# Three of eight inner pairs of a gate-and-up group by seven block products, with half of the weight sums made by an accumulating DMA

## The chip, the cores and the metric

The kernel runs on one core of one Trainium2 chip. TensorE multiplies, VectorE (DVE) and ScalarE (ACT) work on tiles in SBUF and read the PSUM banks, GpSimd (POOL) here only issues DMAs by software, SyncE (SP) issues DMAs by hardware. The metric is the device time of one execution in microseconds. All data are float32; TensorE works on pairs of rounded parts (below).

## The reference, cut to what matters

One encoder block over 256 tokens of width 2048: four mixers, an attention over a memory of 256 rows, and a gated feed-forward. The change touches only the first half of the last line, the product of the normed tokens with `w_gate_up` (2048 x 11264):

```python
x = x + mix @ w_out[l]
x = x + cross_attention(rms_norm(x, norm_g[l, 1]), mem_n, w_xq[l], w_xkv[l], w_xo[l])
x = x + swiglu(rms_norm(x, norm_g[l, 2]), w_gate_up[l], w_down[l])

def swiglu(h, w_gate_up, w_down):
    gate, up = jnp.split(h @ w_gate_up, 2, axis=-1)
    return (jax.nn.silu(gate) * up) @ w_down
```

## The kernel before, in words

**Weights.** All weight matrices are cut on the host into blocks of 128 x 128, in the order in which they are used, and laid into one array `W` of 252 slabs. A slab is 16 blocks, 128 partitions x 2048 floats, 1 MB. `Stream` brings them in. SP loads a slab into one of three `raw` buffers (line 81). Each half slab (1024 columns) is then split in two: ScalarE copies it rounded to `wh` (line 102), VectorE subtracts to get the rest `wl` (line 103). The pool `wp` holds three such halves. `take` hands out four blocks (512 columns) at a time, and before the first block of each half it has the next two halves made as well; with the pool `extra` open it would be three, with a fourth buffer.

**Products.** The tokens are held transposed, as 16 slots of 128 inner rows, each split the same way: `slot[:, 0:256]` the rounded part of all 256 tokens, `slot[:, 256:512]` the rest. A block product of 128 tokens with 512 columns over 128 inner rows is therefore three matmuls, hi x wh, hi x wl, lo x wh (`part_rows`, lines 349 to 351), all into one PSUM bank.

**Gate and up.** `gate_up` walks over 11 groups of 512 gate columns and the 512 up columns that belong to them. For a group, `gemm_rows` makes the gate columns (16 inner blocks, two banks: tokens 0 to 127 and 128 to 255), `gate` applies Silu on ScalarE (line 882), then the up columns follow in two other banks, and `up` multiplies (VectorE, line 206), transposes in blocks of 32 (line 390) and has POOL store the result to the DRAM array `hidden` (line 392). So a group takes 8 slabs and 8 x 24 = 192 matmuls. Group 0 is done in another order, for its slots arrive late.

**Behind it.** The generator `fetch` reads `hidden` back in 128-token-wide pieces (POOL, line 397) into `tmp` buffers, and ScalarE and VectorE split them into the slots `f` for the product with `w_down`; 28 of 44 are fetched while gate and up still run, the rest at the start of `down`. Such generators are stepped by `Background.poll`, by a count of the work that was recorded. After that the tile layer orders each engine's queue by its own plan; the queue then runs strictly in that order, each instruction waiting for semaphores. PSUM has two pools of four banks: `psG` (`pg`) for the large products, `psM` (`pm`) for the small.

Of the kernel before, what the change touches and what calls it, by code (L numbers as in the profile page):

```python
# [34 lines left out]
CUTS = {0: [0, 256, 512, 1024, 2048]}  # L35
# [25 lines left out]
class Stream:  # L61


    def __init__(self, tc, pools, W, bg):
        self.tc, self.nc, self.W, self.bg = tc, tc.nc, W, bg
        self.rawp, self.wp = pools
        self.order = []
        self.n = 0
        self.after = []
        self.halves = []  # L70
        self.raw = None
        self.extra = None
        self.places = []

    def _half(self):

        nc, n = self.nc, 8 * len(self.halves)
        if n % 16 == 0:
            self.raw = self.rawp.tile([P, 2048], F32, name="raw", tag="raw")
            for a, b in zip(CUTS[n], CUTS[n][1:]) if n in CUTS else [(0, 1024), (1024, 2048)] if self.after else [(0, 2048)]:  # L80
                (nc.scalar if (n, a) == (0, 0) else nc.sync).dma_start(self.raw[:, a:b], self.W[n // 16][:, a:b])
                if self.after:
                    self.after.pop(0)()
# [12 lines left out]
        pool = self.extra if self.extra and len(self.halves) % 4 == 3 else self.wp  # L96
        wh, wl = (pool.tile([P, 1088], F32R, name=t, tag=t) for t in ("wh", "wl"))
        at = 48 if any(a <= n < b for a, b in ROWS) else 8
        wh, wl = wh[:, at:at + 1024], wl[:, at:at + 1024]
        edges = [0, 256, 512, 1024] if n == 0 else [0, 512, 1024] if n == 8 else [0, 1024]  # L100
        for a, b in zip(edges, edges[1:]):
            nc.scalar.copy(wh[:, a:b], r[:, a:b])  # L102
            nc.vector.tensor_tensor(out=wl[:, a:b], in0=r[:, a:b], in1=wh[:, a:b].bitcast(F32), op=ALU.subtract)  # L103
        self.bg.dve(1024)
        self.halves.append((wh, wl))

    def take(self, w, k, c, nb=1):
        if self.n % 8 == 0:
            ahead = self.n // 8 + 1 + min(3 if self.extra else 2, self.n // 16)
            while len(self.halves) < min(ahead, NBLK // 8):  # L110
                self._half()
        half, o = self.halves[self.n // 8], (self.n % 8) * P
        if self.n >= NBLK - HELD:
            (wh, wl), o = half[o // 512], 0
        else:
            wh, wl = half
        self.order += [(w, k, c + i * P) for i in range(nb)]
        self.n += nb
        if self.n % 8 == 0:
            self.halves[self.n // 8 - 1] = None  # L120
        return wh[:, o:o + nb * P], wl[:, o:o + nb * P]


class Background:
# [17 lines left out]
    def first(self, g):  # L142

        self.q.sort(key=lambda e: e[0] is not g)
# [29 lines left out]
class Block:  # L174
# [25 lines left out]
    def tt(self, out, a, b, op):  # L200
        self.bg.dve(math.prod(out.shape[1:]))
        self.nc.vector.tensor_tensor(out=out, in0=a, in1=b, op=op)  # L202
# [139 lines left out]
    def part_rows(self, p, r, slot, wh, wl, start, stop, narrow=False):  # L342

        if narrow:
            for c in (slice(0, R), slice(R, 512)):
                self.part_rows(p[:, c], r, slot, wh[:, c], wl[:, c], start and c.start == 0, stop)
            return
        hi, lo = slot[:, r * P:(r + 1) * P], slot[:, R + r * P:R + (r + 1) * P]
        self.nc.tensor.matmul(p, hi, wh, start=start, stop=False)  # L349
        self.nc.tensor.matmul(p, hi, wl, start=False, stop=False)  # L350
        self.nc.tensor.matmul(p, lo, wh, start=False, stop=stop)  # L351
        self.bg.pe(0.68 * wh.shape[1] / 512)

    def gemm_rows(self, w, cols, slots, done=None, parts=None, before=None, out=None):

# [506 lines left out]
    def mlp(self):  # L862
        tc, nc, act = self.tc, self.nc, self.act
        with tc.tile_pool(name="fp", bufs=1) as fp:
            self.gap(fp, 192)
            f = act[4:12] + [fp.tile([P, 512], F32R, name=f"f{i}") for i in range(20)] + self.h3
# [7 lines left out]
    def gate_up(self, gp, f):  # L874

        nc = self.nc
        box, g, stored = {}, {}, []

        def gate(ps):
            for r in range(2):  # L880
                g[r] = gp.tile([P, 512], F32, name=f"g{r}", tag=f"g{r}")
                nc.scalar.activation(g[r], ps[r], AF.Silu, scale=box["col"][:, r:r + 1])

        def up(j, ps):
            for r in range(2):
                h, u = (gp.tile([P, 512], F32, name=n, tag=n) for n in ("h", "u"))
                self.stt(h, ps[r], box["col"][:, r:r + 1], g[r], ALU.mult, ALU.mult)
                self.store_turned(self.ff, 4 * j, r, u, h)
            stored.append(self.bg.now)

        def fetch(k0, k1, ahead, pause, wait=0):
# [32 lines left out]
        self.bg.drain(col)  # L924
        gate(ps[0])
# [722 lines left out]
```

## Time and profile before

| what | value |
|---|---|
| time, median of 3 runs (lowest, highest) | 1462.64 us (1462.53, 1463.66) |
| span of the profiled execution | 1461.5 us |
| instructions | 17996 |
| TensorE busy | 1452.1 us, 99% |
| VectorE busy | 920.9 us, 63% |
| ScalarE busy | 735.2 us, 50% |
| POOL busy | 207.8 us, 14% |
| moved by DMA | 320.15 MB, 219 GB/s over the span |

The page gives the span of the profiled execution, from its first to its last instruction, and no other time of it; the runs without a profile have a median 1.1 us above that span. Busy time of TensorE (PE) is the union of matmuls that overlap, so the mean duration of one matmul (390 ns) is longer than the distance from one to the next. PEld are the weight loads, which run beside the matmuls. Groups are named by the line of the program that issued them, with what they write and read. A DMA's "to landing" runs from its issue to the arrival of its last byte.

### The profile page before, as it was taken

How to read it: one execution, taken by the hardware profiler on the slowest of the kernel's cores; microseconds unless marked ns; L12 is line 12 of the kernel's file. 1: busy time of each engine (PE TensorE's matmuls, PEld its weight loads, DVE VectorE, ACT ScalarE, POOL GpSimd, SP SyncE). 2: the span in 40 equal slices, each digit the busy share in tenths (PEclk: the TensorE clock that was granted, in tenths of full speed). 3: DMA queues.
4: the chain of work that ended last, by engine and by line, in shares of the span. 5: the costliest groups of instructions: out<-in, count | busy, mean ns of one | idle time of the engine just before them, and what ended most of it. 6: DMA issues, size and time to landing. Idle time of an engine off the chain costs nothing.

```text
span 1461.5 us, 17996 instructions
## 1 busy us (share of the span) xinstructions
PE 1452.1 (99%) x6724; PEld 1206.9 (83%) x6724; DVE 920.9 (63%) x1319; ACT 735.2 (50%) x1048; POOL 207.8 (14%) x276
## 2 busy tenths in 40 slices
PE   9999999999999999999999999999999999999997
PEld 7888888888888888888888888888888888888886
DVE  6668868777887676676665555455555456444445
ACT  7566655447555465565554444444444445434344
POOL 0000100012302333530411110011110011000000
PEclk9999999999999999999999999999999999999999
DMA  9877555456757788864867666666766666555554
GB/s 353 295 284 248 200 200 173 145 202 211 229 185 243 243 251 260 253 209 150 257 227 228 213 218 211 213 215 228 229 206 212 216 217 219 198 193 186 197 201 144
DMA packets 60071, 320.15 MB, mean 219 GB/s; under 512 B 9517, under 2 KB 11214, under 8 KB 28368
## 3 DMA queue, kind: packets, MB, share of 16 engines
q1 hardware_dynamic: 46208, 281.11, 56.0%
q0 software_dynamic: 13344, 37.24, 9.8%
q8 instruction: 52, 0.85, 0.2%
q10 hardware_dynamic: 432, 0.66, 0.1%
q14 instruction: 35, 0.29, 0.1%
HBM read 298.52 MB, written 20.45 MB: 218 GB/s over the span
## 4 chain that ended last, share of the span: by engine, by line
PE 99%; DMA 0%; ACT 0%; SPq 0%; DVE 0%; issue 0%
PE pg L349 29%; PE pg L351 29%; PE pg L350 29%; PE pg L300 4%; PE pg L301 2%; PE pm L1101 1%; PE pm L855 1%; PE pm L351 1%; PE pm L349 1%; PE pm L350 1%; PE pm L826 1%; DMA raw<-in_W 0%; PE pm L1510 0%; PE pm L827 0%; PE pm L1275 0%; PE pm L1062 0%
## 5 line engine op out<-in xcount | busy, mean ns | idle before, releaser
L103 DVE TENSOR_TENSOR wl<-raw,wh 128x1024 fp32r<-128x1024 f32 (+1 forms) x503 | 611.5, 1216 | 477.5 <-ACT wh L102 476.5
L102 ACT CAST wh<-raw 128x1024 fp32r<-128x1024 f32 (+1 forms) x503 | 524.0, 1043 | 597.8 <-PE pg L351 527.5
L349 PE MATMUL pg<-wh,act 128*128 128x512 f32 (+1 forms) x1666 | 650.2, 390 | 0.1
L350 PE MATMUL pg<-wl,act 128*128 128x512 f32 (+1 forms) x1666 | 648.4, 389 | 0.5 <-DVE wl L103 0.5
L351 PE MATMUL pg<-wh,act 128*128 128x512 f32 (+1 forms) x1666 | 648.6, 389 | 0.0
L349 PEld LDWEIGHTS pg<-wh,act 128*128 128x128 f32 x1666 | 313.0, 188 | 66.4 <-issue 1.5
L351 PEld LDWEIGHTS pg<-wh,act 128*128 128x128 f32 x1666 | 312.9, 188 | 65.6 <-DVE act L202 0.2
L350 PEld LDWEIGHTS pg<-wl,act 128*128 128x128 f32 x1666 | 313.0, 188 | 65.1 <-DVE wl L103 1.1
L300 PE MATMUL pg<-act,wh 128*128 128x512 f32 x256 | 90.5, 395 | 0.0
L301 PE MATMUL pg<-act,wl 128*128 128x256 f32 x256 | 71.8, 280 | 0.0
L392 POOL DMA_DIRECT2D hidden<-u x22 | 16.7, 763 | 386.5 <-DVE u L390 386.5
L300 PEld LDWEIGHTS pg<-act,wh 128*128 128x128 f32 x256 | 48.1, 188 | 10.5
L351 PE MATMUL pg<-wh,f 128*128 128x512 f32 x140 | 54.5, 389 | 0.0
L349 PE MATMUL pg<-wh,f 128*128 128x512 f32 x140 | 54.5, 389 | 0.0
L350 PE MATMUL pg<-wl,f 128*128 128x512 f32 x140 | 54.5, 389 | 0.0
L301 PEld LDWEIGHTS pg<-act,wl 128*128 128x128 f32 x256 | 48.2, 188 | 0.2
L397 POOL DMA_DIRECT2D tmp<-hidden x44 | 38.9, 890 | 39.5 <-ACT wh L102 24.3
L392 POOL DMA_DIRECT2D features<-tmp x32 | 22.8, 717 | 95.9 <-DVE tmp L390 95.9
L351 PEld LDWEIGHTS pg<-wh,f 128*128 128x128 f32 x140 | 26.3, 188 | 5.5
L350 PEld LDWEIGHTS pg<-wl,f 128*128 128x128 f32 x140 | 26.3, 188 | 5.4
L349 PEld LDWEIGHTS pg<-wh,f 128*128 128x128 f32 x140 | 26.3, 188 | 5.3
L397 POOL DMA_DIRECT2D ar<-features x24 | 21.1, 888 | 20.7 <-DMA features<-tmp 13.0
(314 smaller groups left out, 1046.0 us busy)
## 6 DMA issues: line engine op xcount, KB each, us to landing
raw<-in_W SPq DMA_DIRECT2D x246, 1024.0 KB, 5.0
raw<-in_W SPq DMA_DIRECT2D x11, 512.0 KB, 7.0
hidden<-u POOLq DMA_DIRECT2D x22, 256.0 KB, 3.5
tmp<-hidden POOLq DMA_DIRECT2D x44, 128.0 KB, 5.1
features<-tmp POOLq DMA_DIRECT2D x32, 128.0 KB, 2.7
ar<-features POOLq DMA_DIRECT2D x24, 128.0 KB, 6.5
k<-in_mem SPq DMA_DIRECT2D x8, 256.0 KB, 7.6
keys<-k POOLq DMA_DIRECT2D x8, 256.0 KB, 7.4
```

What stands on the lines that cost most here:

```text
L102: nc.scalar.copy(wh[:, a:b], r[:, a:b])
L103: nc.vector.tensor_tensor(out=wl[:, a:b], in0=r[:, a:b], in1=wh[:, a:b].bitcast(F32), op=ALU.subtract)
L300: self.nc.tensor.matmul(p[:, :], wh, slot[:, :], start=start, stop=False)
L301: self.nc.tensor.matmul(p[:, 0:R], wl, slot[:, 0:R], start=False, stop=stop)
L349: self.nc.tensor.matmul(p, hi, wh, start=start, stop=False)
L350: self.nc.tensor.matmul(p, hi, wl, start=False, stop=False)
L351: self.nc.tensor.matmul(p, lo, wh, start=False, stop=stop)
L392: self.nc.gpsimd.dma_start(to[r], u.rearrange("p (k c) -> p k c", c=P))
L397: self.nc.gpsimd.dma_start(t.rearrange("p (g t) -> p g t", t=32), src)
L826: nc.tensor.matmul(p[:, :], q[d][:, r * P:(r + 1) * P], kt[d][:, :], start=d == 0, stop=False)
L855: nc.tensor.matmul(p[:, 0:R], v[m][:, s], pt[m][:, c:c + R], start=m == 0 and v is vh and c == 0, stop=m == 1 and v is vl)
L1101: self.b.nc.tensor.matmul(p, a, b, start=start and n == 0, stop=stop and n == 2)
```

## The change

In ten groups (1 to 10), three of the eight slabs are used in another way. For a pair of inner blocks k0, k1 the four weight blocks (k0 and k1, gate and up) and the two token halves form a 2 x 2 by 2 x 2 block product. It is done with seven block products instead of eight. For that, sums of weight blocks and sums of token blocks are needed:

- **Tokens, once.** `combine` makes four sums for each of three pairs (slots 0 to 5) and splits them into tiles `z`.
- **Weights, for each such slab.** The order of blocks within the slab is k1-gate, k0-gate, k1-up, k0-up. SP loads the first 1536 columns into `raw`, and the last 512 columns (k0-up) twice, side by side, into a new tile `two`. A DMA issued by POOL adds columns 512 to 1535 (k0-gate, k1-up) from DRAM onto `two`, which then holds k0-gate + k0-up and k1-up + k0-up. VectorE makes two further sums, in `raw` (in `_sums`, part 2). The slab is then split in four parts of 1024, 512, 1024 and 1024 columns instead of two of 1024.
- **Results.** The seven products go to eight banks in all: four of them shared with the plain products of the group (a0, a1 gate; b0, b1 up), four mixed ones, 1, 5, 6, 7, that belong to several outputs. `mixed` combines these into `g0`, `g1` and two `h` tiles, `gated` adds the gate banks and applies Silu, `upped` adds the up banks.
- **Order.** `GROUP` gives the order of plain (N) and summed (S) slabs: N N S N S N S N. Gate and up are no longer one after the other in a group.
- **Room.** `wp` gets a fourth half buffer from a pool `wy`, so three halves are made ahead in gate and up; `two` has one buffer. Six of the `f` slots now lie in `z`, so 22 pieces of `hidden` instead of 28 are fetched early.

```diff
+GATE_UP = 1920 // 16 + 8
+GROUP = "NNSNSNSN"
+PAIRED = {GATE_UP + 8 * j + i for j in range(10) for i, x in enumerate(GROUP) if x == "S"}
...
+    def _buffers(self, n, m):
+        pool = self.extra if self.extra and len(self.halves) % 4 == 3 else self.wp
+        at = 48 if any(a <= n < b for a, b in ROWS) else 8
+        return (pool.tile([P, 1088], F32R, name=t, tag=t)[:, at:at + m] for t in ("wh", "wl"))
+
+    def _load(self, n):
+        nc = self.nc
+        self.raw = self.rawp.tile([P, 2048], F32, name="raw", tag="raw")
+        if n // 16 in PAIRED:
+            W, t = self.W[n // 16], self.sums.tile([P, 1024], F32, name="two", tag="two")
+            nc.sync.dma_start(self.raw[:, 0:1536], W[:, 0:1536])
+            for a in (0, 512):
+                nc.sync.dma_start(t[:, a:a + 512], W[:, 1536:2048])
+            nc.gpsimd.dma_start(t, W[:, 512:1536], accum_op=ALU.add)
+            self.two = t
+            return
...
+    def _sums(self):
+        nc, r, ph = self.nc, self.raw, self.phase
+        src = (r[:, 512:1536], r[:, 0:512], self.two, r[:, 0:1024])[ph]
+        wh, wl = self._buffers(self.made, src.shape[1])
+        if ph == 2:
+            nc.vector.tensor_tensor(out=r[:, 512:1024], in0=self.two[:, 0:512], in1=r[:, 1024:1536], op=ALU.add)
+            nc.vector.tensor_tensor(out=r[:, 0:512], in0=r[:, 512:1024], in1=r[:, 0:512], op=ALU.add)
+            self.bg.dve(1024, 2)
+        nc.scalar.copy(wh, src)
+        nc.vector.tensor_tensor(out=wl, in0=src, in1=wh.bitcast(F32), op=ALU.subtract)
...
+    def _fill(self):
+        ahead = self.at + 1 + min(3 if self.extra else 2, self.n // 16)
+        while len(self.halves) < ahead and self.made < NBLK:
+            self._half()
...
+    def combine(self, z, a, b):
+        tt, t, u, v, w = self.tt, *(self.tmp() for _ in range(4))
+        for x, y in ((t, a), (u, b)):
+            tt(x, y[:, 0:R].bitcast(F32), y[:, R:512].bitcast(F32), ALU.add)
+        yield SOON
+        tt(v[:, 0:P], t[:, P:R], u[:, P:R], ALU.subtract)
+        tt(w[:, 0:P], t[:, 0:P], t[:, P:R], ALU.subtract)
+        tt(v[:, P:R], v[:, 0:P], t[:, 0:P], ALU.subtract)
+        tt(w[:, P:R], u[:, 0:P], v[:, P:R], ALU.add)
+        yield SOON
+        for i, x in enumerate((v, w)):
+            self.split2(z[:, i * R:i * R + R], z[:, 512 + i * R:512 + i * R + R], x)
...
+    def paired_rows(self, w, cols, slots, sums, plan, mixed, first, hold=None, ready=None):
...
+        count = {"a0": len(rest) + s, "a1": len(rest) + s, "b0": len(rest) + s, "b1": len(rest)}
...
+                pairs = iter((("1", a[0]), ("b0", x4), ("a0", a[1]), ("5", x1), ("7", s3), ("a1", a[2]), ("6", s2)))
+                for parts in st.take_sums(w, ks, cols):
+                    for wh, wl in parts:
+                        name, (hi, lo) = next(pairs)
+                        put(name, hi, lo, wh, wl)
+                        self.bg.poll()
...
-            with tc.tile_pool(name="gp", bufs=2) as gp:
-                self.gate_up(gp, f)
+            with tc.tile_pool(name="wy", bufs=1) as self.st.extra, tc.tile_pool(name="tw", bufs=1) as self.st.sums, \
+                    tc.tile_pool(name="gp", bufs=2) as gp:
+                self.gap(self.st.extra, 64)
+                self.gate_up(gp, f, z)
+                self.st.extra = None
...
+        def mixed(q1, q5, q6, q7):
+            g[0], g[1], h[0], h[1] = (gp.tile([P, 512], F32, name=n, tag=n) for n in ("g0", "g1", "h", "h"))
+            nc.scalar.copy(g[0], q1)
+            self.tt(h[0], g[0], q6, ALU.add)
+            self.tt(g[1], h[0], q7, ALU.add)
+            self.tt(h[0], q5, h[0], ALU.subtract)
+            self.tt(h[1], q5, g[1], ALU.subtract)
+
+        def gated(*ps):
+            for r in range(2):
+                self.tt(g[r], g[r], ps[r], ALU.add)
+                nc.scalar.activation(g[r], g[r], AF.Silu, scale=box["col"][:, r:r + 1])
+
+        def upped(j, ps):
+            for r in range(2):
+                self.tt(h[r], h[r], ps[r], ALU.add)
+            up(j, h, h)
...
+        sums = [((2 * i, 2 * i + 1), z[i]) for i in range(GROUP.count("S"))]
+        comb = self.bg.add(combined())
...
-        early = self.bg.add(fetch(0, FT - 16, 3, 2.0, 15))
+        early = self.bg.add(fetch(0, FT - 22, 3, 2.0, 15))
+        self.bg.drain(comb)
         for j in range(1, DFF // 512):
-            gate(self.gemm_rows("w_gate_up", [j * 512], self.h3)[0])
-            up(j, self.gemm_rows("w_gate_up", [DFF + j * 512], self.h3)[0])
+            upped(j, self.paired_rows("w_gate_up", [j * 512, DFF + j * 512], self.h3, sums, GROUP, mixed, gated))
         self.bg.drain(early)
-        self.bg.add(fetch(FT - 16, FT, 6, SOON))
+        self.bg.add(fetch(FT - 22, FT, 6, SOON))
```

More of the change, by code (lines that the diff above doesn't have):

```diff
@@ L95, in _half @@
             return
[L96 to L99, printed above, removed]
+        wh, wl = self._buffers(n, 1024)
         edges = [0, 256, 512, 1024] if n == 0 else [0, 512, 1024] if n == 8 else [0, 1024]
@@ L119, in take, with take_sums @@
         if self.n % 8 == 0:
-            self.halves[self.n // 8 - 1] = None
+            self._used()
         return wh[:, o:o + nb * P], wl[:, o:o + nb * P]
+    def take_sums(self, w, ks, cols):
+        assert self.n // 16 in PAIRED and self.n % 16 == 0
+        self.order += [(w, ks[k], cols[c] + i * P) for k, c in ((1, 0), (0, 0), (1, 1), (0, 1)) for i in range(4)]
+        for ph in range(4):
+            self._fill()
+            wh, wl = self.halves[self.at]
+            yield [(wh[:, a:a + 512], wl[:, a:a + 512]) for a in range(0, wh.shape[1], 512)]
+            self._used()
+        self.n += 16
 class Background:
@@ L347, in part_rows, with part @@
             return
-        hi, lo = slot[:, r * P:(r + 1) * P], slot[:, R + r * P:R + (r + 1) * P]
+        self.part(p, slot[:, r * P:(r + 1) * P], slot[:, R + r * P:R + (r + 1) * P], wh, wl, start, stop)
+    def part(self, p, hi, lo, wh, wl, start, stop):
         self.nc.tensor.matmul(p, hi, wh, start=start, stop=False)
@@ new lines, in paired_rows, with put @@
+    def paired_rows(self, w, cols, slots, sums, plan, mixed, first, hold=None, ready=None):
+        st, s, nk = self.st, len(sums), len(slots)
+        rest = [k for k in range(nk) if not any(k in ks for ks, _ in sums)]
+        steps = [(c, k) for c in range(2) for k in rest]
+        todo, q = iter(sums), {}
+        count = {"a0": len(rest) + s, "a1": len(rest) + s, "b0": len(rest) + s, "b1": len(rest)}
+        left, total = {}, 0
+        def put(name, hi, lo, wh, wl):
+            if name not in q:
+                q[name] = self.gbank() if name in count else self.bank()
+                left[name] = count.get(name, s)
+            new = left[name] == count.get(name, s)
+            left[name] -= 1
+            self.part(q[name][:, :], hi, lo, wh, wl, new, left[name] == 0)
+        form = lambda t, r: (t[:, r * P:(r + 1) * P], t[:, R + r * P:R + (r + 1) * P])
+        n = done = 0
+        for kind in plan:
+            if kind == "S":
+                ks, z = next(todo)
+                a = [form(slots[ks[0]], 0), form(slots[ks[1]], 0), form(slots[ks[1]], 1)]
+                x1, s2, s3, x4 = ((z[:, i * P:i * P + P], z[:, 512 + i * P:512 + i * P + P]) for i in range(4))
+                pairs = iter((("1", a[0]), ("b0", x4), ("a0", a[1]), ("5", x1), ("7", s3), ("a1", a[2]), ("6", s2)))
[4 more added lines that the diff above has]
+                        self.bg.poll()
+                done += 1
+                if done == s:
+                    mixed(*(q[i] for i in "1567"))
+            else:
+                for c, k in steps[n:n + 4]:
+                    if ready:
+                        ready(k)
+                    wh, wl = st.take(w, k, cols[c], 4)
+                    for r in range(2):
+                        put("ab"[c] + str(r), *form(slots[k], r), wh, wl)
+                        self.bg.poll()
+                n += 4
+            if first and done == s and n >= len(rest):
+                first(q["a0"], q["a1"])
+                first = None
+        assert n == len(steps) and done == s
+        return q["b0"], q["b1"]
```

60 lines of the change are left out of this document (40 added, 20 removed).

## The prediction

> **What bounds the kernel now.** I read the page's busy times and its chain first, then the stretches of gate and up, then the durations by shape, the order in time at a group's seam, and the DMA landings.
>
> ```profile
> span 1461.5 us, 17996 instructions
> ...
> PE 1452.1 (99%) x6724; PEld 1206.9 (83%) x6724; DVE 920.9 (63%) x1319; ACT 735.2 (50%) x1048; POOL 207.8 (14%) x276
> ...
> PE 99%; DMA 0%; ACT 0%; SPq 0%; DVE 0%; issue 0%
> ```
>
> TensorE is never without work and the chain is TensorE alone, so a matmul taken away is time won as long as nothing else comes late. The median of the runs, 1462.6, lies 1.1 above the span; I carry that 1.1 along and sum against 1462.6. Two stretches of one group each, one with pieces of `hidden` coming back and one without, and the instruction that marks a group's end:
>
> ```profile
> core 0: us, PE busy (x) PEld busy (x) DVE busy (x) ACT busy (x) POOL busy (x), PEclk, DMA share, GB/s
> 821.60:865.20 43.60, 43.60 (x194) 36.10 (x193) 23.46 (x26) 19.25 (x22) 5.05 (x6) 1.00 0.67 217
> 1126.30:1169.80 43.50, 43.50 (x193) 36.04 (x192) 22.02 (x22) 18.02 (x18) 5.05 (x6) 1.00 0.67 218
> ```
>
> ```profile
> L206 DVE SCALAR_TENSOR_TENSOR h<-pg,rc,g x22: 740/742/746, 778.1 to 1214.0; 128x512 f32<-128x512 f32 x22
> ```
>
> Ten groups in 1214.0 - 0.7 - 778.1 = 435.2: 43.5 a group, 192 matmuls, 0.2266 each. VectorE works 23.4 of it. What holds the splits back is TensorE, which frees the half buffers:
>
> ```profile
> ACT wh L102 <- PE pg L351: 214.2, 136, 1.7
> ```
>
> **The gain.** Each S slab has 21 matmuls instead of 24: 30 x 3 = 90 fewer, 90 x 0.2266 = 20.4 us, 2.04 a group; a group becomes 183 x 0.2266 = 41.5. A plain half lasts TensorE 2.72, the four parts of an S slab 1.36, 0.68, 1.36, 1.36 (4.76 together).
>
> **What VectorE and ScalarE get.**
>
> ```profile
> L103 DVE TENSOR_TENSOR wl<-raw,wh 128x1024 fp32r<-128x1024 f32 x498 | 608.7, 1223 | 474.8 <-ACT wh L102 473.8
> L103 DVE TENSOR_TENSOR wl<-raw,wh 128x512 fp32r<-128x512 f32 x3 | 2.0, 690 | 2.7 <-ACT wh L102 2.7
> L202 DVE TENSOR_TENSOR k<-k,k 128x512 f32<-128x512 f32 x24 | 16.4, 685 | 0.7 <-DMA keys<-k 0.4
> L202 DVE TENSOR_TENSOR res<-res,pg 128x512 f32<-128x512 f32 x23 | 14.8, 676 | 3.4 <-PE pg L351 3.4
> L202 DVE TENSOR_TENSOR f<-tmp,f 128x256 fp32r<-128x256 f32 x20 | 8.4, 418 | 0.0
> L202 DVE TENSOR_TENSOR w3l<-pm,w3h 128x128 fp32r<-128x128 f32 x8 | 2.3, 283 | 0.0
> L102 ACT CAST wh<-raw 128x1024 fp32r<-128x1024 f32 x498 | 521.6, 1048 | 595.1 <-PE pg L351 527.5 <-PE pg L300 26.1 <-PE pm L351 20.9
> L882 ACT ACTIVATE g<-pg,rc 128x512 f32<-128x512 f32 x22 | 15.1, 690 | 10.6 <-PE pg L351 10.6
> ```
>
> Each row gives the mean of one shape. A group on VectorE: ten plain halves 12.2; three S slabs at 3 x 1.223 + 0.690 + two sums 2 x 0.685 = 5.73, 17.2; `mixed`, `gated`, `upped` eight sums at 0.68, 5.4; the multiply and transpose 2.7; four splits of `hidden` pieces 1.7. Sum 39.2 of 41.5, 95%, where it was 54%. ScalarE gets 19 copies of 1024 columns and three of 512, 19 x 1.05 + 3 x 0.69 (the Silu row as bound for 512 columns), one bank copy 0.7, two Silu 1.4, four splits at 0.42, 25.8 in all, 62%: covered. So VectorE's mean fits, but its queue is in order, and what counts is the seam.
>
> **The seam.** As the changed program is built, VectorE's queue runs, from the last S slab on: N7's halves, the next group's first half, `mixed`, second half, three more of `mixed` and the first of `gated`, third half, second of `gated`, the two `upped` sums, multiplies, transposes, fourth half, then the S slab. Two pairs there take 1.40 and 1.29:
>
> ```profile
> 821.62 1.40 DVE L206 SCALAR_TENSOR_TENSOR h<-pg,rc,g 128x512 f32<-128x512 f32 x2
> 822.94 1.29 DVE L390 STREAM_TRANSPOSE u<-h 128x512 f32<-128x512 f32 x2
> 824.15 1.18 DVE L103 TENSOR_TENSOR wl<-raw,wh 128x1024 fp32r<-128x1024 f32 x1
> ```
>
> Let TensorE end a group at 0. A half can be split when TensorE has used the one four before it (four buffers), then takes 1.05 on ScalarE and 1.22 on VectorE. N7's first half follows part 1 of the S slab, used up at -8.84: ready at -6.6, the next two one after the other at -5.4 and -4.1. `mixed` 1 ends -3.5, the half -2.2, four sums +0.5, the half 1.7, `gated` 2.4 (TensorE, which after the reordering begins with ten matmuls for the other bank, wants that bank at 2.27: 0.1 late), `upped` 3.7, multiplies 5.2, transposes 6.4, fourth half 7.7 (wanted 8.16), S parts 1 and 2 at 8.9 and 9.6, a split 10.0, a sum 10.7, part 3 at **11.9**, second sum 12.6, its copy 13.6, part 4 at 14.9. Wanted at 14.28: 0.6 late, 0.2 in groups without the split. I take 0.4 a group, 4 us (ends 0 and 10).
>
> **The step that decides: `two`.** It has one buffer. From the end of part 3 (both readers done) the next summed slab waits for: SP's two loads of 256 KB, POOL's adding DMA, two sums and a split. The prices:
>
> ```profile
> raw<-in_W SPq DMA_DIRECT2D x246, 1024.0 KB, 5.0
> ...
> hidden<-u POOLq DMA_DIRECT2D x22, 256.0 KB, 3.5
> ...
> keys<-k POOLq DMA_DIRECT2D x8, 256.0 KB, 7.4
> ...
> gg<-in_gkw SPq DMA_DIRECT2D x1, 256.0 KB, 2.6
> ```
>
> ```profile
> L81 SPq DMA_DIRECT2D raw<-in_W x73: 327/328/328, 821.7 to 1213.4; - x73
> ...
> DMA to landing us min/median/max: 4.7/5.0/7.2
> ```
>
> ```profile
> 823.93 1.52 POOL L392 DMA_DIRECT2D hidden<-u  x2 [35.16 <-DVE u L390]
> 828.83 3.53 POOL L397 DMA_DIRECT2D tmp<-hidden  x4 [3.38 <-DMA hidden<-u]
> ```
>
> Loads: 2.6 plus one issue 0.33 = 2.9. Hand-overs: the first transpose ends at 822.94 + 0.65 = 823.59, POOL starts at 823.93, 0.3; two of them 0.6. Sums and split 2 x 0.685 + 1.22 = 2.6. So a turn is 6.1 + A, with A the adding DMA. No row has one. Lower end: 3.5, a POOL store of half its size. Upper end: 7.4 (the slow POOL row), plus 0.8 for 256 KB more ((5.0 - 2.6) / 3) and 1.6 for reading 512 KB of old values back, 9.8. An addition needs both operands, so 1 MB is read: nearest is the 1 MB load, 5.0, plus 0.9 for POOL against SP (3.5 - 2.6), 5.9. Bytes in a group go from 217 GB/s to (5 x 1 + 3 x 1.75 MB + 1 MB of `hidden`) / 41.5 = 284, so I add a quarter of the way from 5.0 to 7.2, 0.6: **A = 6.5**.
> [...]
>
> Distance available: part 3 of the third S slab is wanted at 10.88 + 2 x 10.2 + 2.04 = 33.3, with the 0.4 33.7; from 11.9 that is 21.8 for two turns. Two turns need 2 x 12.6 = 25.2: 3.4 late a group, 34 us. Behind the waiting sum on VectorE stand the next halves, so TensorE runs its lead down and waits. The third turn, over the seam, has 21 us alone. On SP the `two` loads stand behind a `raw` load and before another whose buffer is freed later anyway; POOL's stores and four reads of `hidden` take 832.36 - 823.93 = 8.4 (the rows above), so from 6.1 to 14.5, and the loads land at 15.1. Both cost nothing; with that cover gone (a seam 1 later) the reads would add what they overrun.
>
> **The rest.** `combine`: 3 x (4 x 0.42 + 4 x 0.28) = 8.4 on VectorE beside four slabs of group 0 that leave about as much; I take 2 (ends 0 and 8.4). Six more pieces at the start of `down`, 6 x 0.42 on VectorE, have 22 x 6 x 0.2266 = 30 us of TensorE before they are wanted: 0. The first `two` load is moved ahead in SP's queue and waits for the last attention head; the `raw` load behind it is wanted two slabs, 10.9, later and needs 5.0 + 2.3: 0.
>
> Sum: 1462.6 - 20.4 + 4 + 34 + 2 = **1482**.
>
> **Rivals.**
> *The adding DMA costs like a plain copy, faster.* A = 3.5 + 0.8 = 4.3, a turn 10.4, two 20.8 of 21.8: hidden. 1462.6 - 20.4 + 4 + 2 = 1448 (1442 with seam and opening at nothing). It decides up to A = 4.8; even is reached at A = 5.5. For it: at a DMA share of 0.67 the weight loads land in 5.0 where their best is 4.7, so there is room. Against: the second operand.
> [...]
> *The adding DMA is slow, much slower.* A = 9.8: two turns 31.8, 10 late: 1548. For it: three more DMAs a summed slab beside the weights, and `keys` at 7.4.
> *VectorE becomes the bound at the seam.* `two` in time, but whatever moves the third half past -4.1 comes out one for one, for the bank of `gated` has no margin there. Hand-overs of 0.3 that I left out between ScalarE's copy and VectorE, three on this stretch, make 1 a group, 10 us: 1458; it stands even with before at 1.4 a group. Range 1452 to 1464. For it, 95%; against it, a lead of three halves.
>
> **How the numbers follow.** `two` late by my sum 0.45 (A 5.9 to 7.4: 22 to 52 us late, 1470 to 1500); copy-like 0.28; slow 0.15; VectorE 0.12. Anything within 3 us, 0.2%, counts as the same. Faster 0.28 + half of VectorE's, 0.34; same 0.05; slower 0.61. The range runs from 1444, just above the best of the copy case, to 1518, which leaves out most of the slow one.
>
> **What would show it.** Right: TensorE gaps twice in a group, ended by the split of `two`; VectorE's longest wait at the first sum, for the POOL DMA; a landing of 6 to 7 us for that DMA. Wrong: that landing at or below 4.8 (then 1448), TensorE waits at the seam instead, or matmuls not 0.2266 apart.

## The result, and the profile after

The changed kernel takes **1572.07 us** in the median of four runs (1569.46 to 1573.89), against 1463.09 (1462.53 to 1463.66): ratio 1.0745, 95% interval 1.073 to 1.076. The profiled execution has a span of 1570.7. Forecast were 1482, 1444 to 1518: the direction was right, the time lies outside the range.

The page of the changed kernel, its busy times and the chain:

```profile
span 1570.7 us, 18471 instructions
...
PE 1481.3 (94%) x6634; PEld 1214.9 (77%) x6634; DVE 1059.8 (67%) x1543; ACT 785.8 (50%) x1124; POOL 234.3 (15%) x306
...
PE 25%; DMA 7%; issue 5%; DVE 3%; ACT 1%; SPq 0%; POOLq 0%; DVEq 0%; ACTq 0%
DMA two<-in_W 7%; PE pg L415 7%; PE pg L416 7%; PE pg L417 7%; DVE wl L142 2%; PE pm L416 2%; PE pm L417 1%; PE pm L415 1%; ACT wh L141 1%; DVE raw L138 1%; SPq L95 0%; DVE wl L128 0%; ACT res L1130 0%; DVE f L265 0%; ACT pm L1110 0%
```

TensorE has 90 matmuls fewer, as counted, and is no longer always at work. The chain, which was TensorE alone, now has the transfers into `two` as its first line. (Its shares add up to 41% of the span: the profile follows it back to 920 us only, which takes in the last seven of the ten groups.) The landing times of those transfers and of the weights, and the instruction that marks a group's end (two in a group, 0.6 apart):

```profile
raw<-in_W SPq DMA_DIRECT2D x216, 1024.0 KB, 5.2
raw<-in_W SPq DMA_DIRECT2D x30, 768.0 KB, 6.2
two<-in_W SPq DMA_DIRECT2D x60, 256.0 KB, 3.6
two<-in_W POOLq DMA_DIRECT2D x30, 512.0 KB, 8.6
```

```profile
L265 DVE TENSOR_TENSOR h<-h,pg x20: 679/680/683, 833.2 to 1323.6; 128x512 f32<-128x512 f32 x20
```

A group takes (1323.6 - 0.6 - 833.2) / 9 = 54.4 us; it was 43.5, and 41.5 was wanted. Ten times 10.9 is the whole loss of 109. VectorE, SP and POOL in the order of time, in one group; the number in brackets is the idle time before:

```profile
887.33 0.68 DVE L265 TENSOR_TENSOR g<-g,pg 128x512 f32<-128x512 f32 x1
...
894.51 0.68 DVE L138 TENSOR_TENSOR raw<-two,raw 128x512 f32<-128x512 f32 x1
895.80 1.23 DVE L142 TENSOR_TENSOR wl<-two,wh 128x1024 fp32r<-128x1024 f32 x1 [0.62 <-ACT wh L141]
...
911.91 0.69 DVE L138 TENSOR_TENSOR raw<-two,raw 128x512 f32<-128x512 f32 x1 [7.18 <-issue]
...
913.25 1.22 DVE L142 TENSOR_TENSOR wl<-two,wh 128x1024 fp32r<-128x1024 f32 x1
...
927.86 0.69 DVE L138 TENSOR_TENSOR raw<-two,raw 128x512 f32<-128x512 f32 x1 [7.57 <-issue]
```

```profile
897.06 1.46 SPq L95 DMA_DIRECT2D two<-in_W  x2
900.08 0.33 SPq L100 DMA_DIRECT2D raw<-in_W  x1
902.68 0.33 SPq L93 DMA_DIRECT2D raw<-in_W  x1
914.50 0.81 SPq L95 DMA_DIRECT2D two<-in_W  x2
915.97 2.60 SPq L100 DMA_DIRECT2D raw<-in_W  x2
930.43 0.81 SPq L95 DMA_DIRECT2D two<-in_W  x2
```

```profile
903.99 0.93 POOL L96 DMA_DIRECT2D two<-in_W  x1 [3.09 <-DVE wl L142]
920.81 0.88 POOL L96 DMA_DIRECT2D two<-in_W  x1 [15.89 <-DVE wl L142]
```

One can follow a turn of `two` here. The split of part 3 ends at 897.03 and SP issues the loads at 897.06. POOL issues the adding DMA 6.9 later, the first sum starts 7.9 after that, and the split ends 2.6 later: 17.4. The next turn is 6.3 + 7.05 + 2.6 = 15.9. What VectorE, at the first sum, and TensorE see of it (who waited for whom: total, times, longest):

```profile
DVE raw L138 <- issue: 91.5, 12, 8.4
DVE raw L138 <- DMA two<-in_W: 60.0, 8, 8.2
PE pm L415 <- ACT wh L141: 62.0, 20, 4.3
PE pm L416 <- DVE wl L142: 16.0, 20, 1.0
```

Twenty waits, two in each group, as forecast; the third turn, over the seam, has time enough: VectorE is never idle before its first sum. ("issue" means that the profile names no releaser. For eight of VectorE's twenty waits it names the transfer, and the other twelve stand at the same place.) After 19 of TensorE's 20 waits its matmuls run at half their rate for a while, at a granted clock of 0.50 over 3.4 or 6.8 us. Stretches of 8 us around the first wait (length, then busy times, the granted clock, DMA share, GB/s):

```profile
904.00:912.00 8.00, 5.60 (x25) 4.32 (x23) 0.82 (x3) 0.02 (x1) 0.92 (x1) 1.00 0.86 243
912.00:920.00 8.00, 5.97 (x18) 4.63 (x19) 7.97 (x10) 6.25 (x8) 0.00 (x0) 0.79 0.42 125
```

The clock at 0.79 was in no step of the forecast. Its first explanation was that it costs some 5 us a group on top of the waits; an experiment below decides that.

### The profile page after: what moved, and what is told of

It is laid out like the page before. It is cut to its first block, busy times and chain, and to the rows that moved or that the text cites. A ratio compares the mean times of both kernels' runs of the same rounds, so it can differ in the third digit from the quotient of the medians.

```text
span 1570.7 us, 18471 instructions
## 1 busy us (share of the span) xinstructions
PE 1481.3 (94%) x6634; PEld 1214.9 (77%) x6634; DVE 1059.8 (67%) x1543; ACT 785.8 (50%) x1124; POOL 234.3 (15%) x306
## 3 DMA queue, kind: packets, MB, share of 16 engines
q0 software_dynamic: 17664, 52.97, 14.3%
## 5 line engine op out<-in xcount | busy, mean ns | idle before, releaser
L415 PE MATMUL pg<-wh,act 128*128 128x512 f32 (+1 forms) x1486 | 585.0, 395 | 1.9 <-DVE g L265 1.9
L416 PE MATMUL pg<-wl,act 128*128 128x512 f32 (+1 forms) x1486 | 583.9, 393 | 0.2
L417 PE MATMUL pg<-wh,act 128*128 128x512 f32 (+1 forms) x1486 | 582.6, 392 | 0.0
L415 PEld LDWEIGHTS pg<-wh,act 128*128 128x128 f32 x1486 | 283.1, 190 | 63.2 <-DVE g L265 2.3
L416 PEld LDWEIGHTS pg<-wl,act 128*128 128x128 f32 x1486 | 282.7, 190 | 60.0 <-DVE wl L128 1.4
L417 PEld LDWEIGHTS pg<-wh,act 128*128 128x128 f32 x1486 | 282.1, 190 | 59.8 <-DVE act L265 0.2
L141 ACT CAST wh<-two 128x1024 fp32r<-128x1024 f32 x30 | 31.4, 1046 | 194.8 <-DMA two<-in_W 119.3
L138 DVE TENSOR_TENSOR raw<-two,raw 128x512 f32<-128x512 f32 x30 | 20.7, 690 | 151.5 <-issue 91.5
L415 PE MATMUL pm<-wh,z 128*128 128x512 f32 x96 | 48.9, 510 | 62.0 <-ACT wh L141 62.0
L142 DVE TENSOR_TENSOR wl<-raw,wh 128x1024 fp32r<-128x1024 f32 (+1 forms) x90 | 92.3, 1044 | 17.5 <-ACT wh L141 16.0
L96 POOL DMA_DIRECT2D two<-in_W x30 | 26.5, 884 | 374.7 <-DVE wl L142 158.3
L415 PEld LDWEIGHTS pm<-wh,z 128*128 128x128 f32 x96 | 23.4, 244 | 75.2 <-ACT wh L141 70.4
L416 PE MATMUL pm<-wl,z 128*128 128x512 f32 x96 | 50.4, 525 | 16.0 <-DVE wl L142 16.0
L417 PE MATMUL pm<-wh,z 128*128 128x512 f32 x96 | 47.3, 493 | 0.0
```

Source lines behind the costliest of these rows:

```text
L96: nc.gpsimd.dma_start(t, W[:, 512:1536], accum_op=ALU.add)
L138: nc.vector.tensor_tensor(out=r[:, 512:1024], in0=self.two[:, 0:512], in1=r[:, 1024:1536], op=ALU.add)
L141: nc.scalar.copy(wh, src)
L142: nc.vector.tensor_tensor(out=wl, in0=src, in1=wh.bitcast(F32), op=ALU.subtract)
```

## The experiments

A time without a range in brackets is that of a single execution. Some of the runs leave out bytes, a transfer or a sum that the result needs; of these the time alone counts. In the decompositions below, each number is the mean over ten groups, worked out from the order of time of VectorE and POOL in the same way as above. "Turn 1" goes from the first S slab of a group to the second, "turn 2" from the second to the third; a group runs from the `h` row.

### Without the transfers

```diff
-            W, t = self.W[n // 16], self.sums.tile(...)
...
-            for a in (0, 512):
-                nc.sync.dma_start(t[:, a:a + 512], W[:, 1536:2048])
-            nc.gpsimd.dma_start(t, W[:, 512:1536], accum_op=ALU.add)
-            self.two = t
+            self.two = self.raw[:, 512:1536]
```

> Edit: the three transfers into the tile two (two plain loads and the adding DMA) are left out; the third half and the sums of the fourth are made from columns 512 to 1535 of raw itself. So half of the weight sums are missing from the numbers; all matmuls, copies, subtractions and raw loads stay. Theory 'the turn of two': without the transfers no part 3 waits, a group falls from 54.4 to 41.5-42.5 us and the granted clock in the groups goes back to 0.99: 1572 - 10 x 12 = about 1450 us (1440 to 1460). Rival 'seam': VectorE's queue (39 us busy in a group) or the narrow parts bound the group, and the transfers only fill what is left: 1475 us or more. Rival 'matmul side': the new matmuls and their weights' order cost the clock by themselves: 1500 us or more, with granted clock near 0.9 in the groups.

Measured: 1445.4 us. The group's row:

```profile
L262 DVE TENSOR_TENSOR h<-h,pg x20: 678/681/683, 824.2 to 1198.1; 128x512 f32<-128x512 f32 x20
```

(1198.1 - 0.6 - 824.2) / 9 = 41.5, the sum of the matmuls, with a granted clock of 0.997 over the span. VectorE, the seam and the new kind of product cost next to nothing; everything that was lost came with the transfers. The two rivals fall.

### Two buffers

```diff
-        self.tp = pool("tp", 11)
+        self.tp = pool("tp", 10)
...
-... tc.tile_pool(name="tw", bufs=1) as self.st.sums
+... tc.tile_pool(name="tw", bufs=2) as self.st.sums
```

> Edit: two buffers for the tile two instead of one (and one buffer of 2 KB less for down outputs, 10 in place of 11). Theory 'the turn of two': loads and adding DMA of the next slab no longer wait until part 3 of the last has let go; they still stand behind the next raw load on SP. The transfers of a slab then take 6 (raw) + 7 to 8.6 (adding) = about 14 us against 12 us until part 3 wants them: 1450 to 1500 us, likeliest 1475. Rival 'transfers': the DMA engines are too full (2.25 MB of reads and writes for a slab, 4-KB packets of double length), so a second buffer only lets them collide earlier: 1540 us or more, with the adding DMA landing later than its 8.6 us.

> Edit: two buffers for the tile two, a second time, now timed in rounds beside the others: 1449 to 1453 us, ratio to the kernel before 0.991 to 0.993. The theory of turns asks for 1445 to 1452; a time above 1455 would speak against it.

Measured: 1451.0 in the first run, then **1447.07** (1446.33 to 1449.45) in rounds, ratio to the kernel before 0.989, 95% interval 0.9875 to 0.9904. A version that is 1.1% faster than the kernel before, clear of the spread of the runs, and a little below what was expected of the second run. Its landing times and its group:

```profile
two<-in_W SPq DMA_DIRECT2D x60, 256.0 KB, 4.8
two<-in_W POOLq DMA_DIRECT2D x30, 512.0 KB, 9.4
```

```profile
L265 DVE TENSOR_TENSOR h<-h,pg x20: 675/679/682, 822.8 to 1198.6; 128x512 f32<-128x512 f32 x20
```

All transfers into `two` land later than in the changed kernel, and a group takes 41.7. So it isn't how long they take, but that one buffer puts them in a row with the splits. The loads of a slab now start a whole turn earlier, 17 to 30 us ahead of the first sum, and VectorE is idle before none of these sums. The rival of full DMA engines falls.

### Fewer turns, and turns further apart

```diff
-GROUP = "NNSNSNSN"
+GROUP = "NNSNNNSN"    # two_pairs
+GROUP = "NSNNSNNS"    # spread
```

> Edit: two S slabs in a group (places 3 and 7) in place of three (3, 5, 7), one buffer for two as in the changed kernel. Theory 'turns': one turn of two takes 16 to 18 us, and the group needs as many turns as it has S slabs; three turns of 18 make the 54 us that the changed kernel and the spread order both took, two make 36 and fit into the 43.5 - 2 x 0.68 = 42.1 us of a group with two S slabs: no part 3 waits, the clock stays at 0.99 or more, 1462.6 - 10 x 1.36 = 1449 us, and a few tenths a group for the seam: 1449 to 1456. Rival 'each adding DMA costs': the slowdown of the changed kernel is 36 us for each S slab's place in the groups (110 / 3 of them), two cost 2/3 of it: 1462.6 + 73 = about 1535 us. Between the two, 1470 to 1500, neither holds.

> Edit: two S slabs in a group with one buffer for two, timed in rounds: 1449 to 1453 us, ratio 0.990 to 0.993. The theory of turns asks for 1449 and a little; a time above 1456 would speak against it.

> Edit: the three S slabs of a group stand at places 2, 5 and 8 in place of 3, 5 and 7, so that 16 to 17 us of matmuls (three slabs) lie from one part 3 to the next twice and 11 us once, in place of 11 us twice and 20 us once. Theory 'the turn of two': a turn of 16.0 to 17.4 us no longer fits only at the one short distance; instead of two waits of about 3.5 us a group has one of 3 to 4 and perhaps one below 1, and the clock falls half as often: 1572 - 10 x (5 to 9) = 1480 to 1520 us. Rival 'total transfers': what counts is the sum of the bytes in a group, not their distance: 1555 us or more.

Measured: two pairs 1450.5, in rounds 1450.24 (1449.01 to 1450.95), ratio 0.991 (0.9893 to 0.9922), one buffer kept. Two thirds of the summed slabs and none of the loss: it goes by turns, not by adding DMAs.

The spread order came to 1562.8, and I had expected 1480 to 1520. The time is in the rival's range, yet its reason (bytes alone) is refuted by the two buffers, which move the same bytes. The turns were 19.2, 18.4 and 16.0; any three turns in a row add up to a group, and the row of the group gives (1312.3 - 0.6 - 830.2) / 9 = 53.5:

```profile
L265 DVE TENSOR_TENSOR h<-h,pg x20: 674/678/681, 830.2 to 1312.3; 128x512 f32<-128x512 f32 x20
```

In this order the transfers come late in the third turn too: VectorE is idle before its first sum for 0.1 to 1.0 us in eight of ten groups, where in the changed kernel it was not. My expectation held the turn at 16 to 17.4; in turn 1 the adding DMA took 11.1 to the first sum instead of 9.35, with raw loads of 768 KB and 1 MB issued up to 2.5 us ahead of it and a third raw load 1.3 to 4.3 behind.

### Is the clock a loss of its own?

```diff
+                    if ph == 1 and done:
+                        for _ in range(16):
+                            self.nc.tensor.matmul(q["a1"], self.zero, z[:, 0:512], start=False, stop=False)
```

> Edit: sixteen matmuls with a stationary tile of zeros (they add nothing to bank a1) ahead of part 3 of the second and third S slab in each group, 16 x 0.2266 = 3.6 us each, which is about the wait that stands there; everything else is the changed kernel, two turns of 16 to 18 us included. Theory 'clock by waits': TensorE is not idle for 3 to 4 us any more, the granted clock in the groups goes from 0.90 to 0.98 or more, and the group loses only its waits (41.5 + 7.6 = 49 to 50.5 us in place of 54.4): 1520 to 1540 us. Rival 'clock by something else' (transfers, kind of matmul): the clock stays near 0.9 and the added matmuls come on top or nearly: 1565 to 1600 us. Rival 'three turns bound': the clock goes up, but the group stays at three turns of 18: 1560 to 1575 us with a clock of 0.98.

Measured: 1578.4, granted clock 0.991. One of the two stretches of the wait, and the group:

```profile
912.00:920.00 8.00, 6.74 (x28) 4.87 (x27) 7.33 (x9) 6.07 (x8) 0.00 (x0) 1.00 0.34 88
```

```profile
L265 DVE TENSOR_TENSOR h<-h,pg x20: 678/680/684, 833.3 to 1330.0; 128x512 f32<-128x512 f32 x20
```

The clock is back at 1.00 and nothing is won: a group takes 55.1, its turns 17.5 and 16.6. **My theory that the slow clock costs 5 us a group falls.** TensorE at half rate only spent time in which it would have waited for the next turn. The third theory holds, with the time 3 us above its range.

### What a turn is made of

Five runs change the transfers. One takes the addition away (the copy alone), one makes the two loads one, one leaves the loads out (the two lines with a minus go), one makes them small, one halves the raw loads of the N slabs. In the runs without loads and with small ones `two` is one tile, cleared once.

```diff
-            nc.gpsimd.dma_start(t, W[:, 512:1536], accum_op=ALU.add)
+            nc.gpsimd.dma_start(t, W[:, 512:1536])                            # plain_copy
...
-            for a in (0, 512):
-                nc.sync.dma_start(t[:, a:a + 512], W[:, 1536:2048])
+            nc.sync.dma_start(t.rearrange("p (a c) -> p a c", a=2),           # one_load
+                              W[:, 1536:2048].unsqueeze(1).to_broadcast([P, 2, 512]))
+            for a in (0, 512):
+                nc.sync.dma_start(t[:, a:a + 32], W[:, 1536:1568])            # small_loads
...
+        if GATE_UP <= n // 16 < GATE_UP + 80:                                 # half_raw
+            nc.sync.dma_start(self.raw[:, 0:1024], self.W[n // 16][:, 0:1024])
```

> Edit: the POOL DMA copies in place of adding (no sum, so half of the weight sums are missing); its wait for the two plain loads stays. Theory 'the adding itself doubles its packets': it lands some 1.5 to 2 us earlier, each of the two turns in a group is 1.5 to 2 us shorter, and with it a little of the clock's loss: 1572 - 10 x (3 to 5) = 1525 to 1542 us. Rival 'issue and landing': the price is the wait, the issue on POOL and the fixed part of a DMA, not the adding: 1560 us or more, and a landing time near 8 us.

> Edit: the two plain loads of 256 KB (the same columns twice) are one transfer of 512 KB that reads them twice. Theory 'turn': the second load lands 5.3 to 6.0 us after its turn began where 2.9 were reckoned; one transfer of 512 KB without an issue of its own for the second half lands in 4 to 5, so each turn is shorter by 1 to 2 us and a group by two to three times that: 1572 - 10 x (2 to 5) = 1520 to 1550 us. Rival: the transfer is as long as both (DMA engines, not issue, are the limit): within 10 us of 1572.

> Edit: the two plain loads ahead of the adding DMA are left out; two is one tile, set to zero once, and the adding DMA adds onto what is there (half of the weight sums are wrong). The adding DMA waits for the last reader of two as before. Theory 'two terms of the turn were too small, the loads most': of a turn of 17.4 us in the changed kernel 6.9 pass from the release to the issue of the adding DMA, 7.9 to its landing, 2.6 in sums and split; without the loads it is issued 0.3 to 0.5 us after the release and the turn is 10.5 to 11.5 us against 10.2 that matmuls need from part 3 to part 3: a wait of 0.3 to 1.3 us twice in a group, 1447 + 10 x (0.6 to 2.6) = 1452 to 1475 us. Rival 'the adding DMA alone is too long beside raw': it lands 10 us or later, as it does with two buffers, and the turn stays at 13 or more: 1500 us or more.

> Edit: the two plain loads into two bring 32 columns each (16 KB) in place of 512 (256 KB); two is one tile, set to zero once, and the adding DMA adds onto what is there (half of the weight sums are wrong). Theory 'the loads take long by their bytes': a small load lands in 2 to 2.6 us, the adding DMA is issued about 3 us after the release where POOL is free and 3.9 where its queue still issues the transfers of the hidden rows (as in the run without loads); turns of about 15.5 and 12 us, a group of 47 to 49 us, 1490 to 1515 us. Rival 'fixed time of a load in this place': the adding DMA is still issued 6 us or later after the release, turns of 16 and more: 1555 us or more.

> Edit: in the ten groups the five N slabs load only their first 1024 columns (512 KB in place of 1 MB) and use them for both halves, so these weights are wrong; matmuls, copies, subtractions, the S slabs and all transfers into two stay. Theory 'shared DMA engines': with half of the raw bytes beside it the second plain load lands in 3 to 4 us in place of 5.3 to 6.0 and the adding DMA in 6.5 to 7; the adding DMA is issued 4 to 5 us after the release; turns of 13 to 14.5 us against 10.2 wanted, a group of 47.5 to 50 us: 1500 to 1530 us. Rival 'the transfers into two take their time by themselves': landing times as in the changed kernel (3.6 and 8.6 in the middle), turns of 16 to 17.4: 1555 us or more.

Measured, in us (release of `two` to the issue of the adding DMA, from there to the first sum, from there to the next release):

| run | time | turn 1 | turn 2 |
|---|---|---|---|
| changed kernel | 1572.1 | 5.6 + 9.35 + 2.6 = 17.5 | 6.3 + 7.25 + 2.6 = 16.1 |
| one_load | 1582.6 | 5.6 + 9.5 + 2.6 = 17.7 | 7.0 + 7.1 + 2.6 = 16.7 |
| plain_copy | 1542.5 | 5.4 + 8.4 + 2.6 = 16.3 | 6.2 + 6.1 + 2.6 = 14.8 |
| half_raw | 1552.6 | 5.7 + 8.4 + 2.6 = 16.6 | 5.5 + 7.5 + 2.6 = 15.55 |
| small_loads | 1546.2 | 3.7 + 9.7 + 2.6 = 16.0 | 2.9 + 9.9 + 2.6 = 15.3 |
| no_loads | 1486.6 | 2.8 + 9.0 + 2.7 = 14.5 | 0.3 + 6.2 + 3.3 = 9.8 |

*The addition* costs 1.2 to 1.3 a turn, 0.3 of it in POOL's issue (0.88 against 0.55), somewhat less than the 1.5 to 2 expected; the time lies half a microsecond beyond the range that I had put down. In the trace's packet records a 4096-byte packet of the adding DMA takes 328 ns in the middle, one of the plain copy 159.

*One load for two* was a miss: it is 10 us slower, not 20 to 50 faster, just outside the rival's range too. Its 512 KB land as late as the second of the two loads did in turn 1, and 0.7 later in turn 2.

*Small loads and no loads* are the instructive pair, and both missed both ranges. Almost no bytes differ between them, but the order does. SP and POOL with small loads, turn 2, and the first sum on VectorE:

```profile
908.76 0.81 SPq L99 DMA_DIRECT2D two<-in_W  x2
910.23 2.60 SPq L104 DMA_DIRECT2D raw<-in_W  x2
```

```profile
911.45 0.88 POOL L100 DMA_DIRECT2D two<-in_W  x1 [13.66 <-DVE wl L132]
```

```profile
921.34 0.69 DVE L142 TENSOR_TENSOR raw<-two,raw 128x512 f32<-128x512 f32 x1 [6.11 <-DMA two<-in_W]
```

And without loads:

```profile
892.28 0.87 POOL L98 DMA_DIRECT2D two<-in_W  x1 [10.35 <-DVE wl L144]
```

```profile
893.47 11.16 SPq L102 DMA_DIRECT2D raw<-in_W  x3
```

```profile
898.50 0.69 DVE L140 TENSOR_TENSOR raw<-two,raw 128x512 f32<-128x512 f32 x1 [0.71 <-DMA two<-in_W]
```

With small loads the adding DMA is issued 2.7 after them, and by then SP has issued the first of two raw loads of 1 MB; the first sum starts 9.9 later. Without loads it is issued ahead of the raw load, and the sum starts after 6.2. So what the loads cost, even small, is the place in front of the raw loads: of the 3.4 us that small loads win in turn 2, the adding DMA gives back 2.6. The packet records of the ten groups show it, again in turn 2. Without loads the first packet of the adding DMA comes 1.6 us after its issue, and its packets take 3.8 to 4.2. In the changed kernel the first comes after 2.2 to 3.4, while packets of the raw loads ahead of it still run, and they take 3.5 to 4.9. With small loads, beside the second raw load, they take 5.8 to 7.0 in nine groups. The first turn without loads misses my range for another reason: POOL's queue is busy until 880.03 with the reads of `hidden`, and the release was at 876.1, the end of this split:

```profile
874.84 1.23 DVE L144 TENSOR_TENSOR wl<-two,wh 128x1024 fp32r<-128x1024 f32 x1
```

```profile
877.40 2.65 POOL L531 DMA_DIRECT2D tmp<-hidden  x3 [4.75 <-issue]
880.03 0.97 POOL L98 DMA_DIRECT2D two<-in_W  x1
```

By then SP has issued a raw load, at 879.11, and the first sum comes 9.4 later. In seven of the ten groups turn 1 takes 15.6 to 17.7; in the first and the last two, 10.2 or 10.3.

*Half of the raw bytes* wins only 0.6 to 0.9 a turn, and its time, 1552.6, lies between the two ranges that I had named. So the bytes beside the turn explain a part only; the plain loads still take 5.5 to the issue of the adding DMA.

The packet records show more of these loads. In turn 2 of the changed kernel their first packet comes 0.96 us after the first issue, half of the packets have started after 2.1 to 2.2, the last ends after 4.9 to 5.9 (with half of the raw bytes 4.3 to 5.0), and POOL issues 0.9 to 1.0 later. The first packet of the raw load behind them comes after 2.9 to 3.6. So the second load's bytes follow the first's and take time of their own. At the pace of the first load, 1.2 us, both would bring POOL's issue at 0.96 + 2 x 1.2 + 0.9 = 4.3, an estimate; the other 2 us are spent beside the raw load. How the sixteen engines divide their time between the queues, and why half raw loads save so little of this, stays open.

### The sums made elsewhere

```diff
-            nc.sync.dma_start(self.raw[:, 0:1536], W[:, 0:1536])
-            for a in (0, 512):
-                nc.sync.dma_start(t[:, a:a + 512], W[:, 1536:2048])
-            nc.gpsimd.dma_start(t, W[:, 512:1536], accum_op=ALU.add)
+            nc.sync.dma_start(self.raw, W)
+            for i in range(2):
+                nc.gpsimd.tensor_tensor(out=t[:, i * 512:i * 512 + 512], in0=self.raw[:, 512 + i * 512:1024 + i * 512], in1=self.raw[:, 1536:2048], op=ALU.add)
...
+                # vector_sums: the same two additions by nc.vector, in part 3
```

> Edit: no transfers into two; raw is loaded whole (1 MB in place of 768 KB), and GpSimd makes the two first sums from it (two 128x512 additions), as the rest needs them. Theory 'turn': 1 MB of raw lands in 5.2 to 5.5 us, the two sums on GpSimd take some us in which the first two parts are used (11 us); no part 3 waits if a turn is below 11 us: 1445 to 1458 us. Rival 'GpSimd': its additions take over 5 us each, or VectorE's instructions beside them grow: 1463 us or more, with VectorE's 128x1024 subtraction above 1.22 us.

> Edit: no transfers into two; raw is loaded whole and VectorE makes all four sums (two more additions of 128x512, 0.685 us each, for each S slab). Theory 'VectorE has room': VectorE is busy 36.3 us of a group of 41.85 in the run with two buffers; with 6 x 0.685 = 4.1 more it has 40.4 of 41.5 and the group is 41.5 to 42.5: 1446 to 1456 us. Rival 'seam': at the group's end VectorE is late already by 0.4 us, and the six additions stand ahead of the splits of the next slabs; the group goes by VectorE's chain, 43 us or more: 1460 to 1475 us, with TensorE waiting for wl.

Measured: by GpSimd 1467.0, by VectorE 1453.38 (1452.57 to 1454.96), ratio 0.993 (0.9914 to 0.9947). The group with the sums on VectorE:

```profile
L265 DVE TENSOR_TENSOR h<-h,pg x20: 674/678/680, 822.4 to 1196.9; 128x512 f32<-128x512 f32 x20
```

(1196.9 - 0.6 - 822.4) / 9 = 41.5, so in the groups VectorE does have room for all four sums. That the run is still 6 us behind the two buffers comes from what follows the groups: VectorE splits none of the pieces of `hidden` before 1200.0, behind the last group, and TensorE waits there for such a split, once for 3.3 us. With GpSimd VectorE's own work grows; VectorE and POOL in that run:

```profile
882.53 5.09 DVE L127 TENSOR_TENSOR wl<-raw,wh 128x1024 fp32r<-128x1024 f32 x2
```

```profile
883.02 3.51 POOL L95 TENSOR_TENSOR two<-raw 128x512 f32<-128x512 f32 x2
```

Two splits beside the additions take 5.09 where two take 2.35 without. The rival named there holds.

## Why the prediction was wrong, step by step

- **The gain**, 2.04 a group: right. Without the transfers a group takes 41.5.
- **VectorE** at 39.2 of 41.5: too high. With two buffers it is busy 323.66 of 375 us, 36.0 of a group of 41.7, mostly because instructions of one queue overlap (two splits of 1.22 take 2.35; the durations of all in this stretch add up to 38.7 a group):

```profile
825.00:1200.00 375.00, 373.93 (x1648) 308.69 (x1647) 323.66 (x383) 212.09 (x246) 60.93 (x71) 1.00 0.90 277
```

  The rival that bounds the seam by VectorE had a chance of 0.12 and is out: without the transfers, and even with six more sums, a group takes 41.5.
- **The seam**: right to about half a microsecond. From the end of the second `gated` sum to the end of part 3, 9.5 was forecast (2.4 to 11.9); in the group above it is 897.03 - 888.01 = 9.0, where the sum ahead of it ends at 888.01. Without the transfers no wait is left there, so the 4 us for it are too much.
- **The turn of `two`**: the mechanism and its place were right, two waits a group, ended by that split, with the longest waits for the POOL DMA. **The step that failed is its price.** 12.6 was reckoned, 17.5 and 16.1 were measured. From the release to the issue of the adding DMA I had 2.9 + 0.3 = 3.2, from the 2.6 of one lone load at 318 us; it was 5.6 and 6.3. The second load stood in this sum with its issue, 0.33, and its bytes at nothing, though they move behind the first's (half of the packets have started after 2.1 to 2.2 us, the last ends after 4.9 to 5.9). From there to the first sum I had A + 0.3 = 6.8; it was 9.35 and 7.25. A came out near only where the DMA is first in line, 6.2 with the hand-over; its landing, 6 to 7 by the forecast, is 8.6 in the middle. That the adding DMA reads a second half megabyte, on which A = 6.5 rested, was my estimate, and no run shows it as bytes: POOL's queue moves 52.97 MB with the 30 adding DMAs and 37.24 without, 15.73 MB or 512 KB for each. What the runs show in its place: packets of 328 ns against 159 in the plain copy, and 1.2 to 1.3 us a turn. What I left out besides is that waiting for the loads puts the adding DMA behind the raw loads. That the raw loads also hold up the plain loads is shown for a small part only, by the run with half of their bytes.
- **The distance**: 21.8 for two turns. With two buffers part 3 follows part 3 in 10.2 and 10.4, 20.6.
- **The sum, with the measured terms**: 33.6 for two turns against 21.8 is 11.8 late, 118 us instead of 34: 1462.6 - 20.4 + 4 + 118 + 2 = 1566. The rest of the forecast's arithmetic reaches the measured 1572 within 6, in part by luck: the distance that is 1.2 too long takes 12 off, and the 4 for the seam and the 2 for `combine` stand against it.
- **Queues and rest at nothing**: SP as said. POOL's reads of `hidden` stay covered in the changed kernel, as said; without the loads they become the 2.8 of turn 1, which is the price that I had named for a lost cover. `combine` and the opening of `down` and the seam can't have cost more than some 3 us together, since the run without the transfers ends 17.3 us before the old kernel.
- **The rivals.** Copy-like: even a real copy in that place leaves 1542, so the addition was never what decided. Slow, 1548 with a landing of 9.8: nearest in time, and in turn 1 nearly its number, but more by way of the loads (2.4 + 3.1 us a group above the forecast) than of the adding DMA (2.55 + 0.45). The clock was in no rival. One of the signs of being wrong, matmuls not 0.2266 apart, did come, behind the waits; the fill shows that it costs nothing here.

## What to carry to other kernels

A chain of transfers through one buffer is priced as a whole turn, from release to release, with the bytes of every load in it, and with each transfer behind what other queues issue while the one before it is under way (from the issue of the adding DMA to the first sum 6.2 us ahead of the raw load, 9.9 behind its issue). The landing time of a lone transfer was the lower end here, not the estimate (2.6 us, where the 256 KB loads of the changed kernel took 2.9 to 6.0). The cure that pays is to take the chain off the reuse of the buffer (a second one, 1447 us, or fewer uses, 1450), since faster transfers in it (no addition, smaller loads, half of the neighbours' bytes) gave back 20 to 30 of 109 us each. Before a slow clock after waits is counted as a loss, fill the wait: if the clock recovers and the time doesn't (0.967 to 0.991 over the span, 1572 to 1578 us here), the wait is set elsewhere.

## What the hardware showed that I had not expected

- After a wait of 3.5 us, and a second one of about 1, TensorE's matmuls of 512 columns ran 0.43 us apart instead of 0.2266:

```profile
913.08 0.49 PE L415 MATMUL pm<-wh,z 128*128 128x512 f32 x1 [3.47 <-ACT wh L141]
914.52 0.80 PE L416 MATMUL pm<-wl,z 128*128 128x512 f32 x1 [0.95 <-DVE wl L142]
915.12 0.63 PE L417 MATMUL pm<-wh,z 128*128 128x512 f32 x1
915.54 0.63 PE L415 MATMUL pm<-wh,z 128*128 128x512 f32 x1
```

  From 914.6 to 917.8 the granted clock was 0.50. The half rate followed 19 of the 20 waits, the shortest of them 2.1 us, at once or up to 1.1 us after TensorE was back at work, and stayed away after one of 2.3. What sets it off beside the length of a wait, these runs don't show.
- VectorE's subtraction of two SBUF tiles went from 1.2 to between 2.3 and 2.5 us beside GpSimd's addition of two SBUF tiles: in the run with the sums by GpSimd two subtractions took 5.09, 4.56 and 4.55 us, where two take 2.35 without. Why, the run doesn't show.
- The adding DMA, 6.5 by my sum, landed in 8.6 in the middle, 5.9 at the least. With the plain copy in its place the first sum still started 8.4 and 6.1 us after the issue, against 9.35 and 7.25 with the addition, in both runs beside raw loads.
